# Feed-forward up-projections of a two-block transformer kernel in seven block products in place of eight

## The chip, the cores and the metric

The kernel runs on one core of a Trainium2 chip. The metric is the device time of one execution in microseconds (us), the median of three runs. Inside the core, five engines work side by side, each with its own queue of instructions in a fixed order: PE (TensorE, matrix products), DVE (VectorE), ACT (ScalarE), POOL (GpSimd) and SP, which issues the loads.

## The reference, cut to what matters

Four layers follow one another on one sequence of 512 tokens of width 1024, in 32-bit floats. The first two layers each have a mixer and a feed-forward; the change is in the two feed-forwards:

```python
def conv_ffn(x, w_up, conv_w, conv_b, w_down):      # x: 512 x 1024
    a, g = jnp.split(x @ w_up, 2, axis=-1)          # w_up: 1024 x 5632
    g = causal depthwise convolution of width 3 over tokens (g) + conv_b
    return (jax.nn.gelu(g) * a) @ w_down            # w_down: 2816 x 1024
```

(The line of the convolution is abridged.)

## The kernel before, in words

Every 32-bit value is held as a pair hi + lo of the matrix engine's rounded type, and every product is three matmuls: hi·hi, hi·lo, lo·hi (`mm3`, L273 to L278). The activations stand transposed as `xh`, `xl` (8 k-blocks of 128 rows, 512 tokens).

Weights arrive as *units* of 1 MB in one of two `raw` buffers. `pump` (L180) loads the next unit when a buffer is free and splits the next *piece* of it into hi and lo: ACT casts (L238), DVE subtracts (L242). At most five pieces exist at a time, the one that PE uses among them; `get` (L254) gives one back and fetches the next. The whole order is written out by hand: each engine works off its queue in the order in which the Python code issues.

In `ffn` (L1127) the 22 chunks of 128 hidden columns are taken two at a time: first the unit of the gate g, then that of the values a, each with two pieces (a piece is one chunk, 1024 x 128). `fm` (L282) multiplies a piece with all 512 tokens into one PSUM bank. `g_evac` (L1134) then scales on ACT (L1137), adds the two shifted taps on DVE (L1138, L1139), applies gelu on ACT (L1140); `a_evac` (L1143) multiplies on DVE (L1145) and splits the product into hi and lo (`split`, L371 and L372). After 12 chunks, and again after the other 10 (`FF_PARTS`), `tm` (L317) and `out_proj` multiply the chunks with the down-projection's weights and add into the residual. The first four chunks of a layer are done for tokens 0 to 255 and then 256 to 511 (`fms` with `split`), since the layer norm ahead of them delivers its tiles one after the other (L405 to L425).

Of the kernel before, what the change touches and what calls it, by code (L numbers as in the profile page):

```python
# [12 lines left out]
F32R = mybir.dt.float32r  # L13
# [6 lines left out]
ALPHA = (2 * 2) ** 0.25  # L20
# [8 lines left out]
SPL = 4  # L29
# [8 lines left out]
def run(gen):  # L38
    for _ in gen:
        pass  # L40
# [73 lines left out]
class Core:  # L114
# [4 lines left out]
    def __init__(self, ctx, tc, io):  # L119
        self.tc, self.nc, self.io = tc, tc.nc, io  # L120
        nc = tc.nc
        self.V, self.A, self.G, self.T = nc.vector, nc.scalar, nc.gpsimd, nc.tensor
        pool = lambda n, **k: ctx.enter_context(tc.tile_pool(name=n, **k))
        self.const = pool("const", bufs=1)
        self.wp = pool("weights", bufs=1)
        self.xp = pool("xt", bufs=1)
        self.sp = pool("slots", bufs=1)
        self.small = pool("small", bufs=4)
        self.pp = pool("psum", bufs=1, space=bass.MemoryType.PSUM)
        self.dp = pool("dram", bufs=1, space=bass.MemoryType.DRAM)  # L130
# [6 lines left out]
        self.live = deque()  # L137
        self.nm = 0
        self.pending = deque()

# [35 lines left out]
    def piece(self, u, view, a, b, direct=False):  # L176
        self.units[u]["left"] += 1
        self.plist.append((u, view, a, b, direct))

    def pump(self, split=True):  # L180
        while True:
            moved = False
            n = self.next_raw
            if n < len(self.units) and (n < self.NRAW or self.units[n - self.NRAW]["left"] == 0):
                raw = self.wp.tile([128, 2048], F32, tag="raw", name=self.name("raw"), bufs=self.NRAW)
                self.units[n]["tile"] = raw
                if self.units[n]["zero"]:
                    self.G.memset(raw[:, :self.units[n]["zero"]], 0.0)
                for dst, src in self.units[n]["srcs"]:
                    self.nc.sync.dma_start(dst(raw), src)  # L190
                    if self.loads:
                        self.loads.popleft()()
                self.next_raw += 1
                moved = True
            n = self.next_piece
            if split and n < len(self.plist) and self.room():
                u, view, a, b, direct = self.plist[n]
# [53 lines left out]
    tight = spare = extra = 0  # L251
    held = 0

    def get(self, n=1):  # L254
# [12 lines left out]
        assert len(self.live) >= n  # L267
        return [(self.live[k][1], self.live[k][2]) for k in range(n)]

    def mm3(self, out, lhs, rhs, start, stop):  # L273
        (lh, ll), (rh, rl) = lhs, rhs
        mm = self.T.matmul
        mm(out, lh, rh, start=start, stop=False)  # L276
        mm(out, lh, rl, start=False, stop=False)  # L277
        mm(out, ll, rh, start=False, stop=stop)  # L278

    step = 8  # L280

# [6 lines left out]
            if k % self.step == self.step - 1:  # L288
                yield self.step * 3 * 216 * (t1 - t0) // 512

    def fms(self, evacs, split=0):


        n = 0
        if split:
            self.flush(1)
            self.extra, self.eager = 0, False
            ws = self.get(split)
            pss = [self.ps() for _ in ws]
            for t0 in (0, 256):  # L300
                for k, (w, p) in enumerate(zip(ws, pss)):
                    if t0 or k == split - 1:
                        self.flush(3 if t0 else 2)
                    yield from self.fm(p, w, t0=t0, t1=t0 + 256)
                    if t0:
                        evacs[k](p)
                        if k == EAGER:
                            self.eager = True
                            self.pump()
            n = split  # L310
        for f in evacs[n:]:
            w, = self.get()
            p = self.ps()
            yield from self.fm(p, w)
            f(p)

    def tm(self, lhs, kpers, n, done, tail=3, pack=False, kind="mm", before=None, extra=2, middle=None):  # L317

# [779 lines left out]
        yield 500  # L1098


    FF_PARTS = (12, 10)

    def ffn_weights(self, l):
        w = self.io["ffn_w_up"][l].rearrange("(k p) n -> p k n", p=128)
        c = 0
        for part in self.FF_PARTS:
            for j in range(c, c + part, 2):
                for base in (D_FF, 0):
                    u = self.unit([(lambda r: r.rearrange("p (k n) -> p k n", k=8), w[:, :, base + 128 * j:base + 128 * j + 256])])
# [15 lines left out]
        self.ffn(1, self.pre_rms)  # L1125

    def ffn(self, l, rms=False):  # L1127
        A, V, al, fr = self.A, self.V, self.al, self.fr
        self.pool_lo = False
        par = self.par[:, l]  # L1130
        c0 = 0
        H = {}

        def g_evac(c, p):  # L1134
# [8 lines left out]
        def a_evac(c, p):  # L1143
            acc = H[c]
            V.tensor_tensor(acc, p, acc, op=MUL)  # L1145
            hi, lo = al(F32R), al(F32R)
            self.split(hi, lo, acc)
            fr(acc)
            H[c] = hi, lo

        for part in self.FF_PARTS:
            fs = []
            for j in range(c0, c0 + part, 2):
                fs += [lambda p, c=c: g_evac(c, p) for c in (j, j + 1)] + [lambda p, c=c: a_evac(c, p) for c in (j, j + 1)]
            run(self.fms(fs, split=SPL if c0 == 0 else 0))
            if c0 == 0:
                gb = self.norm_params(l, 1)
                if rms:
                    g = self.bcast(self.io["norm_pre_2"][0])
                    self.lru_params()  # L1160
                if l == 0 and self.pre_rms:
                    self.table(4)
            lhs = lambda k, i: [t[:, i * 128:i * 128 + 128] for t in H[c0 + k]]
            first = c0 == 0
            if first:
                for h in range(2):
                    run(self.tm(lhs, [2] * (part // 2), 512, lambda i, p, h=h: self.residual(i, h, p), tail=0))
            else:
                self.out_proj(lhs, [2] * (part // 2), gb, 1.0, (lambda i: self.rms_pre(i, g)) if rms else None, tail=5, extra=3)
# [966 lines left out]
```

## Time and profile before

| | |
|---|---|
| median of 3 runs | 2002.4 us (1999.98 to 2003.76) |
| the profiled execution, its own time | 1997.43 us |
| its span in the trace | 1995.5 us |
| PE busy | 1947.4 us, 98% |
| DVE, ACT, POOL busy | 50%, 41%, 21% |
| feed-forward, first layer: first load to last load of its weights | 247.8 to 622.8 us |
| feed-forward, second layer | 924.7 to 1286.8 us |

Busy time on PE is drawn from modelled ends of its matmuls, so the distance between starts tells more than the busy share. The loads run ahead of the products by up to two units.

### The profile page before, as it was taken

The numbers are of one execution on the slowest core, as the hardware profiler recorded it, in microseconds if no ns is written. First come the engines' busy times: TensorE is split into PE (matmuls) and PEld (weight loads), VectorE is DVE, ScalarE is ACT, GpSimd is POOL, SyncE is SP. The second block draws the span as 40 slices with busy tenths as digits, with TensorE's granted clock in tenths as the row PEclk, the third lists the DMA queues.
The fourth block names the chain that finished last, engine by engine and source line by source line (L and its number), as shares of the span: only waits on it lengthen the run. The fifth ranks groups of instructions, "written<-read, shape, count | busy, mean of one in ns | idle before, by whom it ended". The sixth has DMA issues, their size and how long they took to land.

```text
span 1995.5 us, 25737 instructions
## 1 busy us (share of the span) xinstructions
PE 1947.4 (98%) x10228; PEld 1623.8 (81%) x10228; DVE 991.2 (50%) x1692; ACT 817.5 (41%) x1451; POOL 417.6 (21%) x368
## 2 busy tenths in 40 slices
PE   8999989999999999999999999999998999999998
PEld 6678868888888988777888888888886888888887
DVE  3553255442444533763655344375667555455443
ACT  3455434331333344784333233256655533333331
POOL 0334441000000264474300000031443211011000
PEclk9999999999999999999999999999999999999999
DMA  6432223232323433111232423232231322222221
GB/s 199 112 115 68 93 84 101 95 127 85 105 85 123 137 99 122 54 49 64 65 116 94 137 85 105 85 106 70 71 89 70 133 85 90 90 85 90 85 75 52
DMA packets 174164, 189.22 MB, mean 95 GB/s; under 512 B 15080, under 2 KB 133662, under 8 KB 174045
## 3 DMA queue, kind: packets, MB, share of 16 engines
q1 hardware_dynamic: 158044, 165.63, 26.2%
q10 hardware_dynamic: 12064, 17.37, 2.9%
q0 software_dynamic: 3936, 4.59, 0.7%
q8 instruction: 80, 1.31, 0.3%
q14 instruction: 40, 0.32, 0.0%
HBM read 182.19 MB, written 6.65 MB: 95 GB/s over the span
## 4 chain that ended last, share of the span: by engine, by line
PE 80%; DVE 8%; ACT 3%; issue 2%; SPq 2%; DMA 2%; POOL 2%; ACTq 0%; DVEq 0%; POOLq 0%
PE p L276 24%; PE p L277 24%; PE p L278 24%; SPq L190 1%; PE p L1545 1%; PE p L1525 1%; PE p L1663 1%; SPq L851 1%; DVE s L1891 1%; POOL lo L240 1%; PE p L391 1%; PE p L786 1%; DVE s L1890 1%; PE p L366 1%; ACT hi L238 0%
## 5 line engine op out<-in xcount | busy, mean ns | idle before, releaser
L276 PE MATMUL p<-xh,hi 128*128 128x512 f32 (+1 forms) x1200 | 457.9, 382 | 0.7 <-ACT xh L371 0.7
L238 ACT CAST hi<-raw 128x1024 fp32r<-128x1024 f32 (+4 forms) x294 | 301.4, 1033 | 382.5 <-PE p L278 307.9
L277 PE MATMUL p<-xl,hi 128*128 128x512 f32 (+1 forms) x1200 | 454.3, 379 | 1.3 <-DVE xl L372 1.3
L278 PE MATMUL p<-xh,lo 128*128 128x512 f32 (+1 forms) x1200 | 454.3, 379 | 0.4 <-DVE lo L242 0.4
L242 DVE TENSOR_TENSOR lo<-raw,hi 128x1024 fp32r<-128x1024 f32 (+2 forms) x212 | 258.7, 1227 | 356.3 <-ACT hi L238 336.8
L276 PE MATMUL p<-hi,s 128*128 128x512 f32 (+1 forms) x728 | 285.7, 392 | 7.5 <-ACT s L371 4.8
L278 PE MATMUL p<-hi,s 128*128 128x512 f32 (+1 forms) x728 | 283.6, 390 | 0.0
L277 PE MATMUL p<-lo,s 128*128 128x512 f32 (+1 forms) x728 | 282.9, 389 | 0.0
L276 PEld LDWEIGHTS p<-xh,hi 128*128 128x128 f32 x1200 | 225.9, 188 | 44.7 <-ACT xh L371 1.4
L278 PEld LDWEIGHTS p<-xh,lo 128*128 128x128 f32 x1200 | 226.0, 188 | 43.1 <-DVE lo L242 0.6
L277 PEld LDWEIGHTS p<-xl,hi 128*128 128x128 f32 x1200 | 226.0, 188 | 42.8 <-DVE xl L372 2.1
L240 POOL TENSOR_TENSOR lo<-raw,hi 128x1024 fp32r<-128x1024 f32 (+3 forms) x82 | 191.2, 2339 | 329.2 <-ACT hi L238 259.6
L422 POOL TENSOR_TENSOR xtok<-xtok,b 128x512 f32<-128x512 f32 x16 | 26.1, 1629 | 712.9 <-ACT xtok L421 371.9
L276 PE MATMUL p<-hi,xh 128*128 128x512 f32 (+3 forms) x480 | 170.1, 354 | 1.5 <-ACT s L841 0.8
L277 PE MATMUL p<-lo,xh 128*128 128x512 f32 (+3 forms) x480 | 169.0, 352 | 0.5 <-DVE lo L242 0.5
L278 PE MATMUL p<-hi,xl 128*128 128x512 f32 (+3 forms) x480 | 168.8, 352 | 0.0
L276 PEld LDWEIGHTS p<-hi,s 128*128 128x128 f32 x728 | 137.1, 188 | 36.9 <-ACT s L371 6.2
L371 ACT CAST s<-s 128x512 fp32r<-128x512 f32 (+1 forms) x100 | 59.1, 597 | 260.8 <-DVE s L1145 122.7
L278 PEld LDWEIGHTS p<-hi,s 128*128 128x128 f32 x728 | 137.1, 188 | 30.0 <-DVE s L372 2.1
L277 PEld LDWEIGHTS p<-lo,s 128*128 128x128 f32 x728 | 137.1, 188 | 26.6
L276 PEld LDWEIGHTS p<-hi,xh 128*128 128x128 f32 x480 | 90.6, 189 | 14.3 <-issue 1.7
L277 PEld LDWEIGHTS p<-lo,xh 128*128 128x128 f32 x480 | 90.6, 189 | 11.7 <-DVE lo L242 0.8
(313 smaller groups left out, 2584.9 us busy)
## 6 DMA issues: line engine op xcount, KB each, us to landing
raw<-in_ffn_w_up_dram SPq DMA_DIRECT2D x44, 1024.0 KB, 5.1
raw<-in_ret_w_in_dram SPq DMA_DIRECT2D x24, 1024.0 KB, 5.1
raw<-in_ffn_w_down_dram SPq DMA_DIRECT2D x20, 1024.0 KB, 5.1
raw<-in_ev_w_in_dram SPq DMA_DIRECT2D x24, 512.0 KB, 5.3
raw<-in_lru_w_in_dram SPq DMA_DIRECT2D x24, 512.0 KB, 5.7
raw<-in_ret_w_out_dram SPq DMA_DIRECT2D x8, 1024.0 KB, 5.0
raw<-in_lru_w_out_dram SPq DMA_DIRECT2D x6, 1024.0 KB, 5.0
s<-in_od_cmp_w_dram ACTq DMA_DIRECT2D x16, 256.0 KB, 4.8
```

The costliest lines, as they stand in the source:

```text
L190: self.nc.sync.dma_start(dst(raw), src)
L238: self.A.copy(dh, x)
L240: self.G.tensor_tensor(dl, x, dh, op=SUB)
L242: self.V.tensor_tensor(dl, x, dh, op=SUB)
L276: mm(out, lh, rh, start=start, stop=False)
L277: mm(out, lh, rl, start=False, stop=False)
L278: mm(out, ll, rh, start=False, stop=stop)
L366: self.T.matmul(outs[e][:, :n], q[a][r, i * 128:i * 128 + 128], k[b][r, :n], start=j == 0, stop=j == 2)
L371: self.A.copy(hi, src)
L391: self.T.transpose(p[:, c * 128:(c + 1) * 128], halves[b][:, c * 128:(c + 1) * 128], self.ident)
L422: self.G.tensor_tensor(b, b, gb[0][:, 512:], op=MUL)
L786: T.matmul(o[:, i * 128:i * 128 + 128], st["pt"][:, k * 128:k * 128 + 128], va[k][:, h * 128:h * 128 + 128], start=k == 0, stop=k == i)
```

## The change

For every unit but the two of the first pair of chunks, the 1024 x 256 weights and the 512 tokens are cut in 2 x 2 blocks (k-halves of 512, chunks of 128; token halves of 256), and the four results are formed from seven block products in place of eight. A product is 4 k-blocks x 3 matmuls of 256 tokens. In the order of issue (`fm7`) they are: x (first half of k, first tokens), z, e, y, a second accumulation into x (here *s2*), the last product of the unit before (*s4*), a third accumulation into x (*s3*).

- **Weights.** A unit has three pieces: p0 (chunk 0 as it is), and after `post` has overwritten the raw buffer with sums on POOL (four subtractions of 128 x 512), p1 and p2. The lower right block ("corner") is split apart, for s4.
- **Activations.** Once per layer, `sum_steps` forms quarter sums of x on POOL and DVE (a11, a12, a21, a22, then s1 to s4) and splits s1 to s4.
- **Results.** x is copied out of PSUM by ACT after its first, second and third product (t0, t1, t1's second half), and DVE adds z, e and y. The evacuations then read from SBUF: the taps on DVE, and the multiplication of `a_evac` on POOL in place of DVE.
- **Parts.** The down projection follows after 6, 8 and 8 chunks in place of 12 and 10.

```diff
...
+    def seven(self, u):
+        v = lambda r: r.rearrange("p (k n) -> p k n", k=8)
+        def post(r):
+            w = v(r)
+            b11, b12, b21, b22 = w[:, :4, :128], w[:, :4, 128:], w[:, 4:, :128], w[:, 4:, 128:]
+            h, l = self.al(F32R), self.al(F32R)
+            self.split(h.rearrange("p (k n) -> p k n", k=4), l.rearrange("p (k n) -> p k n", k=4), b22)
+            self.corner.append((h, l))
+            self.G.tensor_tensor(b11, b12, b11, op=SUB)
+            self.G.tensor_tensor(b12, b22, b12, op=SUB)
+            self.G.tensor_tensor(b22, b22, b11, op=SUB)
+            self.G.tensor_tensor(b21, b21, b22, op=SUB)
+        for c, f in ((0, post), (0, None), (128, None)):
+            self.piece(u, lambda r, c=c: v(r)[:, :, c:c + 128], 8, 128, post=f)
...
-            if split and n < len(self.plist) and self.room():
+            if split and most and n < len(self.plist) and self.room():
...
+                        if post is not None:
+                            post(raw)
+                        most -= 1
...
-        self.pump()
+        self.pump(most=max(most, n - len(self.live)))
...
+            return [lambda: whole(G, "a11", 0, 0), lambda: whole(G, "a12", 0, 1)]
+        return [lambda: whole(G, "a21", 1, 0), lambda: whole(V, "a22", 1, 1),
+                lambda: comb(V, "s1", "a21", "a22", ADD, "a22"), lambda: comb(G, "s3", "a11", "a21", SUB, "a21"),
+                lambda: part("s1"), lambda: comb(G, "s2", "s1", "a11", SUB, "a11"), lambda: fr(*self.qs.pop("s1")),
+                lambda: part("s2"), lambda: comb(G, "s4", "a12", "s2", SUB, "a12"), lambda: fr(*self.qs.pop("s2")),
+                lambda: part("s3"), lambda: fr(*self.qs.pop("s3")), lambda: part("s4"), lambda: fr(*self.qs.pop("s4"))]
...
+        def mm(p, b, x, start=True):
+            for k in range(4):
+                self.mm3(p[:, :256], (b[0](k), b[1](k)), x(k), start and k == 0, k == 3, on=not start)
+            return 12 * 120
+        def blk(w, r):
+            return [lambda k, t=t: t[:, 4 * r + k] for t in w]
+        def last(u):
+            corner, y, t1, f = u
+            mm(y, [lambda k, t=t: t[:, 128 * k:128 * k + 128] for t in corner], s("s4"), False)
+            V.tensor_tensor(t1[:, :256], t1[:, :256], y[:, :256], op=ADD)
+            self.fr(*corner)
+            f(t1)
+        before = None
+        for u in range(0, len(evacs), 2):
+            w, = self.get(most=0)
+            x, z = self.ps(), self.ps()
+            t0, t1 = self.al(), self.al()
+            yield mm(x, blk(w, 0), a(0, 0))
+            A.copy(t0[:, :256], x[:, :256])
+            yield mm(z, blk(w, 1), a(0, 1))
+            V.tensor_tensor(t0[:, :256], t0[:, :256], z[:, :256], op=ADD)
+            w, = self.get(most=1)
+            y, e = self.ps(), self.ps()
+            yield mm(e, blk(w, 1), a(1, 1))
+            self.steps()
+            yield mm(y, blk(w, 0), s("s1"))
+            w, = self.get(most=1)
+            yield mm(x, blk(w, 1), s("s2"), False)
+            A.copy(t1[:, :256], x[:, :256])
+            if before:
+                last(before)
+                yield 12 * 120
+            self.pump(most=1)
+            yield mm(x, blk(w, 0), s("s3"), False)
+            A.copy(t1[:, 256:], x[:, :256])
+            V.tensor_tensor(t0[:, 256:], t1[:, 256:], e[:, :256], op=ADD)
+            V.tensor_tensor(t1[:, 256:], t1[:, 256:], y[:, :256], op=ADD)
+            evacs[u](t0)
+            before = self.corner.popleft(), y, t1, evacs[u + 1]
+        last(before)
...
-    FF_PARTS = (12, 10)
+    FF_PARTS = (6, 8, 8)
...
+                    if j:
+                        self.seven(u)
+                        continue
...
-            V.tensor_tensor(acc, p, acc, op=MUL)
+            (G if slot else V).tensor_tensor(acc, p, acc, op=MUL)
...
-            run(self.fms(fs, split=SPL if c0 == 0 else 0))
+            n = SPL if c0 == 0 else 0
+            if n:
+                run(self.fms(fs[:n], split=n, sums=True))
...
+            run(self.fm7(fs[n:]))
...
```

The queues show what moves. In them line numbers are those of the changed file. First ACT in the second part of the first layer, before: three units of two pieces; `p` are PSUM banks, `hi` cast weights, `s` slots in SBUF.

```order
L1137 ACTIVATE s717_4416<-p716_4391,par_106 128x512 [waits PE_49]
L1140 ACTIVATE s717_4416<-s717_4416 128x512 [waits DVE_49,Activation_49]
L238 CAST hi718_4421<-raw700_4285 128x1024
L1137 ACTIVATE s722_4452<-p721_4427,par_106 128x512 [waits PE_49]
L1140 ACTIVATE s722_4452<-s722_4452 128x512 [waits DVE_49,Activation_49]
L238 CAST hi723_4457<-raw710_4355 128x1024 [waits DMAHW2_49]
L371 CAST s726_4487<-s717_4416 128x512 [waits DVE_49]
L238 CAST hi728_4491<-raw710_4355 128x1024 [waits PE_49]
```

The same queue with the change, in the same part, from the evacuation of a g chunk (L1280, L1283) to the third copy from PSUM:

```order
L1280 ACTIVATE s722_4282<-s696_4064,par_106 128x512 [waits DVE_49]
L1283 ACTIVATE s722_4282<-s722_4282 128x512 [waits DVE_49,Activation_49]
L262 CAST hi723_4287<-raw703_4125 128x1024 [waits DMAHW0_49]
L511 CAST s725_4291<-raw703_4125 128x512
L450 COPY s714_4193<-p711_4190 128x256 [waits PE_49]
L511 CAST s727_4315<-s710_4185 128x512 [waits Pool_49]
L434 COPY s731_4321<-p729_4319 128x256 [waits PE_49]
L262 CAST hi733_4349<-raw703_4125 128x1024
L262 CAST hi737_4379<-raw703_4125 128x1024 [waits PE_49]
L444 COPY s732_4322<-p729_4319 128x256 [waits PE_49]
```

A cast that waits for POOL (L511 of s710, an a chunk) now stands ahead of the copy of x out of PSUM (L434).

POOL has no row in this part before; its queue with the change, at the same place:

```order
L193 TENSOR_TENSOR raw703_4125<-raw703_4125 128x4x128 [waits DMAHW0_49,DVE_49]
L194 TENSOR_TENSOR raw703_4125<-raw703_4125 128x4x128 [waits Pool_49]
L195 TENSOR_TENSOR raw703_4125<-raw703_4125 128x4x128 [waits DVE_49,Pool_49]
L196 TENSOR_TENSOR raw703_4125<-raw703_4125 128x4x128 [waits Pool_49]
L1290 TENSOR_TENSOR s710_4185<-s713_4192,s710_4185 128x512 [waits DVE_49,PE_49]
L1290 TENSOR_TENSOR s722_4282<-s714_4193,s722_4282 128x512 [waits DVE_49]
```

The multiplication that the cast of s710 waits for stands behind the four subtractions of unit raw703, whose p0 ACT casts just ahead.

PE with the change, the end of product y and the start of s2 of one unit:

```order
L303 MATMUL p717_4224<-s538_3002,lo698_4092 128x256
L301 MATMUL p711_4190<-s543_3040,hi701_4121 128x256 [waits Activation_49]
L302 MATMUL p711_4190<-s545_3042,hi701_4121 128x256
L303 MATMUL p711_4190<-s543_3040,lo702_4122 128x256
```

The second accumulation into the bank of x waits for ACT's copy. In all, PE's queue grows from 9281 rows to 10721 (rows that repeat count once).

## Rows read from the trace of the kernel before

**Rows 1.** The page, part 1: busy time, share of the span, instructions.
```profile
PE 1947.4 (98%) x10228; PEld 1623.8 (81%) x10228; DVE 991.2 (50%) x1692; ACT 817.5 (41%) x1451; POOL 417.6 (21%) x368
```
**Rows 2.** Busy time of each engine in 70 us of up-projection.
```profile
core 0: us, PE busy (x) PEld busy (x) DVE busy (x) ACT busy (x) POOL busy (x), PEclk, DMA share, GB/s
330.00:400.00 70.00, 70.00 (x310) 57.98 (x309) 36.47 (x41) 26.71 (x35) 0.00 (x0) 1.00 0.32 105
```
**Rows 3.** Timeline of PE, matmuls of 512 tokens; the first and the last of 37.
```profile
start us, us, engine line op out<-in xcount [idle before <-releaser]
379.62 0.39 PE L278 MATMUL p<-xh,lo 128*128 128x512 f32 x1
...
387.78 0.39 PE L278 MATMUL p<-xh,lo 128*128 128x512 f32 x1
```
**Rows 4.** Timeline of PE, matmuls of 256 tokens: first and last of 86.
```profile
315.78 0.28 PE L277 MATMUL p<-xl,hi 128*128 128x256 f32 x1
...
325.98 0.28 PE L278 MATMUL p<-xh,s 128*128 128x256 f32 x1
```
**Rows 5.** Timeline of ACT in the up-projection.
```profile
339.65 0.63 ACT L1140 ACTIVATE s<-s 128x512 f32<-128x512 f32 x1 [1.66 <-DVE s L1139]
340.19 1.03 ACT L238 CAST hi<-raw 128x1024 fp32r<-128x1024 f32 x1
...
343.37 0.63 ACT L371 CAST s<-s 128x512 fp32r<-128x512 f32 x1 [2.15 <-DVE s L1145]
```
**Rows 6.** Timeline of DVE in the up-projection.
```profile
336.52 1.23 DVE L242 TENSOR_TENSOR lo<-raw,hi 128x1024 fp32r<-128x1024 f32 x1 [1.70 <-ACT hi L238]
338.02 0.75 DVE L1138 SCALAR_TENSOR_TENSOR s<-p,par,s 128x511 f32<-128x511 f32 x1 [0.28 <-ACT s L1137]
338.81 0.75 DVE L1139 SCALAR_TENSOR_TENSOR s<-p,par,s 128x510 f32<-128x510 f32 x1
...
344.03 0.69 DVE L372 TENSOR_TENSOR s<-s,s 128x512 fp32r<-128x512 f32 x1 [0.69 <-ACT s L371]
```
**Rows 7.** Groups of instructions by line and shape: copies of 256 columns from PSUM.
```profile
L1533 ACT COPY s<-p 128x256 f32<-128x256 f32 x12 | 4.5, 372 | 5.3 <-PE p L1525 5.1
...
L1533 DVE COPY s<-p 128x256 f32<-128x256 f32 x12 | 5.1, 424 | 7.8 <-PE p L1525 6.9 <-POOL s L1518 0.8
```
**Rows 8.** Groups by line and shape: POOL, two operands of 512 columns.
```profile
L1970 POOL TENSOR_TENSOR s<-s,s 128x512 f32<-128x512 f32 x8 | 10.3, 1292 | 60.5 <-DVE s L1969 60.5
...
L240 POOL TENSOR_TENSOR s<-raw,s 128x512 fp32r<-128x512 f32 x8 | 10.1, 1290 | 0.0
```
**Rows 9.** Timeline of POOL during a layer norm.
```profile
947.38 5.04 POOL L240 TENSOR_TENSOR s<-raw,s 128x512 fp32r<-128x512 f32 x4
952.37 1.75 POOL L422 TENSOR_TENSOR xtok<-xtok,b 128x512 f32<-128x512 f32 x1
```
**Rows 10.** Timeline of DVE during the same layer norm.
```profile
951.10 1.86 DVE L424 SCALAR_TENSOR_TENSOR xtok<-xtok,mv,b 128x512 f32<-128x512 f32 x1
...
954.60 0.68 DVE L405 SCALAR_TENSOR_TENSOR xtok<-xtok,p 128x512 f32<-128x512 f32 x1
...
956.88 0.74 DVE L424 SCALAR_TENSOR_TENSOR xtok<-xtok,mv,b 128x512 f32<-128x512 f32 x1
```
**Rows 11.** Timeline of PE around its longest wait for another engine.
```profile
256.38 0.66 PE L994 MATMUL p<-s,s 128*64 128x128 f32 x8 [3.72 <-ACT s L985]
...
257.56 1.12 PE L994 MATMUL p<-s,s 128*64 128x128 f32 x8
...
259.65 1.12 PE L994 MATMUL p<-s,s 128*64 128x128 f32 x8
...
261.38 0.66 PE L994 MATMUL p<-s,s 128*64 128x128 f32 x8
```
**Rows 12.** Timeline of POOL ahead of the first feed-forward.
```profile
305.77 2.15 POOL L423 TENSOR_TENSOR xtok<-xtok,b 128x512 f32<-128x512 f32 x1
```
**Rows 13.** Timeline of PE: its second token half of the first four chunks begins.
```profile
314.62 0.39 PE L277 MATMUL p<-xl,hi 128*128 128x256 f32 x1 [0.34 <-DVE xl L372]
```

More of the change, by code (lines that the diff above doesn't have):

```diff
@@ L137, in __init__ @@
         self.live = deque()
+        self.corner = deque()
+        self.todo = deque()
         self.nm = 0
@@ L174, in unit, with piece, pump @@
         return len(self.units) - 1
-    def piece(self, u, view, a, b, direct=False):
+    def piece(self, u, view, a, b, direct=False, post=None):
         self.units[u]["left"] += 1
-        self.plist.append((u, view, a, b, direct))
-    def pump(self, split=True):
+        self.plist.append((u, view, a, b, direct, post))
+    def seven(self, u):
[12 more added lines that the diff above has]
+            self.piece(u, lambda r, c=c: v(r)[:, :, c:c + 128], 8, 128, post=f)
+    def pump(self, split=True, most=1000):
         while True:
@@ L289, in fm, with fms @@
                 yield self.step * 3 * 216 * (t1 - t0) // 512
-    def fms(self, evacs, split=0):
+    def fms(self, evacs, split=0, sums=False):
         n = 0
@@ L296, in fms @@
             self.flush(1)
+            if sums:
+                self.todo.extend(self.sum_steps(True))
+                self.steps()
             self.extra, self.eager = 0, False
@@ L303, in fms @@
                         self.flush(3 if t0 else 2)
+                    if t0 and k == 0 and sums:
+                        self.todo.extend(self.sum_steps(False))
+                        self.steps(4)
                     yield from self.fm(p, w, t0=t0, t1=t0 + 256)
@@ L306, in fms @@
                         evacs[k](p)
+                        if k:
+                            self.steps(3)
                         if k == EAGER:
@@ L315, in fms, with quarter, sum_steps, whole @@
             f(p)
+    def quarter(self, x, th, kh):
+        return x[:, 4 * kh:4 * kh + 4, 256 * th:256 * th + 256]
+    def sum_steps(self, early):
+        V, G, al, fr = self.V, self.G, self.al, self.fr
+        v = lambda t: t.rearrange("p (k n) -> p k n", k=2)
+        if early:
+            self.qs, self.sums = {}, {}
+        def whole(E, n, th, kh):
+            self.qs[n] = [al(), al()]
+            for c, t in enumerate(self.qs[n]):
+                x = [self.quarter(y, th, kh)[:, 2 * c:2 * c + 2] for y in (self.xh, self.xl)]
+                E.tensor_tensor(v(t), x[0], x[1], op=ADD)
+        def comb(E, n, a, b, op, out):
+            for x, y, t in zip(self.qs[a], self.qs[b], self.qs[out]):
+                E.tensor_tensor(t, x, y, op=op)
+            self.qs[n] = self.qs.pop(out)
+        def part(n):
+            hs, ls = [al(F32R), al(F32R)], [al(F32R), al(F32R)]
+            for h, l, t in zip(hs, ls, self.qs[n]):
+                self.split(h, l, t)
+            self.sums[n] = hs, ls
+        if early:
+            return [lambda: whole(G, "a11", 0, 0), lambda: whole(G, "a12", 0, 1)]
[4 more added lines that the diff above has]
+                lambda: part("s3"), lambda: fr(*self.qs.pop("s3")), lambda: part("s4"), lambda: fr(*self.qs.pop("s4"))]
@@ new lines, in steps, with fr_sums, fm7, a @@
+    def steps(self, n=1000):
+        while n and self.todo:
+            self.todo.popleft()()
+            n -= 1
+    def fr_sums(self):
+        for hs, ls in self.sums.values():
+            self.fr(*hs, *ls)
+    def fm7(self, evacs):
+        V, A = self.V, self.A
+        def a(th, kh):
+            return lambda k: (self.quarter(self.xh, th, kh)[:, k], self.quarter(self.xl, th, kh)[:, k])
+        def s(n):
+            hs, ls = self.sums[n]
+            return lambda k: tuple(t[k // 2][:, 256 * (k % 2):256 * (k % 2) + 256] for t in (hs, ls))
+        def mm(p, b, x, start=True):
[22 more added lines that the diff above has]
+            yield mm(e, blk(w, 1), a(1, 1))
+            self.steps()
+            yield mm(y, blk(w, 0), s("s1"))
[13 more added lines that the diff above has]
+        last(before)
@@ L1141, in g_evac, with a_evac @@
             H[c] = acc
-        def a_evac(c, p):
+            if slot:
+                fr(p)
+        def a_evac(c, p, slot=False):
             acc = H[c]
-            V.tensor_tensor(acc, p, acc, op=MUL)
+            (G if slot else V).tensor_tensor(acc, p, acc, op=MUL)
+            if slot:
+                fr(p)
             hi, lo = al(F32R), al(F32R)
@@ L1162, in ffn @@
                     self.table(4)
+            run(self.fm7(fs[n:]))
+            if c0 + part == 22:
+                self.fr_sums()
             lhs = lambda k, i: [t[:, i * 128:i * 128 + 128] for t in H[c0 + k]]
-            first = c0 == 0
-            if first:
+            alpha = ALPHA if c0 == 0 else 1.0
+            if c0 + part < 22:
                 for h in range(2):
-                    run(self.tm(lhs, [2] * (part // 2), 512, lambda i, p, h=h: self.residual(i, h, p), tail=0))
+                    run(self.tm(lhs, [2] * (part // 2), 512, lambda i, p, h=h: self.residual(i, h, p, alpha), tail=0))
             else:
-                self.out_proj(lhs, [2] * (part // 2), gb, 1.0, (lambda i: self.rms_pre(i, g)) if rms else None, tail=5, extra=3)
+                self.out_proj(lhs, [2] * (part // 2), gb, 1.0, (lambda i: self.rms_pre(i, g)) if rms else None, tail=4, extra=3)
             for c in range(c0, c0 + part):
```

18 lines of the change are left out of this document (9 added, 9 removed).

## Prediction

> **What bounds the kernel now.** The page's busy times come first: PE is busy 98% of the span, the others half or less [rows 1]. Then one stretch of up-projection: of 70 us PE is busy 70, at a granted clock of 1.00 (2.4 GHz); DVE has 36 us of work, ACT 27, POOL none [rows 2]. So there PE's own rate is the time, and the others have room. The rate is read from starts, not from durations, which overlap: 36 steps in 8.16 us are 0.2267 us for a matmul of 512 tokens [rows 3], 85 steps in 10.20 us are 0.120 us for one of 256 [rows 4]. Half the tokens cost 53% of the time.
>
> **What PE gains.** A unit now takes 2 chunks x 8 k-blocks x 3 x 0.2267 = 10.88 us. With the change it is 7 products x 12 x 0.120 = 10.08 us (1.44 us a product). Ten of eleven chunk pairs have two such units, in two layers: 40 units, and PE's queue grows by just the 40 x 36 rows that this means. The gain is 40 x 0.80 = 32 us: the upper bound.
> The Trainium skill (TensorE: Matmul & The Clock Gate, "Back-to-back issue gap") gives N/2.4 + 2.5 ns, 215.8 and 109.2 ns, and so 1.19 us a unit and 47 us in all. The rows are 11 ns above that for either width, and the measurement decides.
>
> **What it adds beside PE.** Prices: cast of 1024 columns on ACT 1.03, of 512 0.63 (I take 0.62), gelu or scaling from SBUF 0.63 [rows 5]; subtraction of 1024 on DVE 1.23, a tap 0.75, 512 columns 0.69 [rows 6]; 256 columns from PSUM 0.37 on ACT, 0.42 on DVE [rows 7]; 512 columns on POOL 1.29 [rows 8]. A hand-over between engines is 0.03 to 0.09 us (a cast ends at 344.00 and DVE starts at 344.03, a tap ends at 339.56 and gelu starts at 339.65) [rows 5, 6]; I take 0.05.
> For a g unit and its a unit: POOL does 8 subtractions and 2 multiplications, 12.9 us. DVE's operations with two operands in SBUF are 6 x 1.23, two corners and two halves of chunks at 0.69, and four taps at 0.75 (before they read PSUM): 13.1 us. Those 26.0 us would hide in 20.2 us of PE if the two engines were free of each other. They are not: while POOL ran four operations back to back, DVE's L424 with two SBUF operands took 1.86 us, alone 0.74; POOL's next took 1.75 instead of 1.29; L405, which reads PSUM, took 0.68 beside POOL's work [rows 8 to 10]. So each waits for the other to end. I take it as a full exclusion; the other bound is none.
>
> **The queues.** The order rows show what stands behind what. ACT's copy of x (L434) must come before PE's s2, and 7.2 us of PE's work separate the end of s4 in one unit from s2 in the next. In that stretch ACT's queue holds the gelu of the chunk that s4 finished, the cast of p0 for the unit after the next, and the cast of an a chunk, which waits for POOL's multiplication, which stands behind the four subtractions that wait for p0. In steady state this closes to a ring over the three engines:
> - g unit's last chunk to a copy: gelu 0.63, cast p0 1.03, subtraction 1.23, corner 0.69, POOL 4 x 1.29 and 1.29, cast 0.62, copy 0.37, cast p1 1.03, subtractions p1 and p2 2.46, adding y 0.42: 14.9 us.
> - on from there: POOL's multiplication 1.29, cast 0.62, cast p0 1.03, subtraction 1.23, corner 0.69, POOL 4 x 1.29 with two taps in between 1.50, cast p1 1.03, subtractions 2.46, adding y 0.42, scaling 0.63, two taps 1.50: 17.6 us, and gelu again.
>
> Together 32.5, with 15 hand-overs 33.2 us for a pair of units, against 21.8 now. PE waits in this ring some 7.9 us ahead of s2 of each g unit and 5 us elsewhere. The five pieces do not hide it: a lead delays a ring, it does not shorten it. Without the exclusion the same walk gives 30.6.
>
> **The sum.** A part of 8 units begins with its pieces ready: 9.3 and 12.2 us for the first pair, three rings of 33.2, and 3.9 at the end, since the last s4 waits for the copy that ACT has behind a gelu and a cast: 125.0 us in place of 8 x 10.88 = 87.0, **+38.0**. There are four such parts, +152.
> The first part of a layer has 4 units, and 12 quarter sums on POOL ahead. POOL is free 6.7 us before the second token half begins (305.77 + 2.15 against 314.62) [rows 12, 13]. From there on the walk to s3 of the first unit is: 15 POOL operations, 19.4 us; DVE's a22 and s1, p1 and p2 in between, 5.2; two taps and gelu 2.1; halves of s1 to s4 with the last two a chunks between, 10.1; z, p0 and corner of the next unit 2.3; its subtractions 5.2; a cast and the copy 1.4: 45.7, with hand-overs 46.6. That is 39.9 after the half began; without any wait s3 would start at 18.8. Behind it p0 and p1 are cast in one unit, with the subtractions in between, as the lead is one piece shorter: units of 15.8, 19.1 and 17.9. The part with its 11.5 us of split chunks is 95.2 us where 55.0 stood: **+40.2**, twice, +80.
> Clock: after 3.72 us of waiting PE still ran a group of 8 in 0.66 us, then from 257.56 to 260.77 the same in 1.12, then in 0.66 again [rows 11]: 3.2 us at half rate, 1.2 GHz for 2.4. Behind a long wait s2 and s4 would take 1.6 us longer, of which the ring has 0.45 in hand. I take 1.15 for each of 12 rings, +14; bounds 0 and 1.6 for each of 26 long waits, 42.
> The third down projection adds 8 residual additions on DVE a layer, beside products of 8 x 12 x 0.2267 = 21.8 us on PE in each half: 0; uncovered they would be 8 x 0.69 = 6 us.
> Sum: 152 + 80 + 14 = +246. Against the profiled execution, 1997.4, that is 2243; the median of the three runs is 5 us above it, so I forecast **2248 us**.
>
> **Rivals.**
> 1. *No exclusion*, the queues alone (0.22). Rows 10 show it for a layer norm only, with other operands. Ring 30.6, parts +30.0 and +33.2: +186, 2002.4 + 186 = 2188. With hand-overs of 0.03 and POOL at 1.26 it is +174. The Trainium skill (GPSIMD Engine Reference, "Specifications") says that POOL's access to SBUF is shared with VectorE and contends with instructions with two SBUF inputs; by that rule my forecast, not this rival, holds.
> 2. *Exclusion alone* (0.08): the lead lets the queues run smoothly, and 26.0 us for a pair stay where 21.8 stood: 20 x 4.3 = +85, 2088. Against it: the ring holds no slack that a lead could use.
> 3. *Faster* (0.04): POOL's work goes under. Place: the four subtractions ahead of the multiplication. The ring has ten POOL operations, so it equals today's 21.8 once they take 1.29 - 11.4/10 = 0.15 us each, and shorter ones give up to 32 us: 1971. Only then, or if POOL's a chunk passed the subtractions, would it decide; no row of POOL with two operands of 512 is near that, and its order is fixed.
> 4. *Clock and restarts cost in full* (0.06): +28 on the forecast, 2276; with POOL at 1.35 some 2290.
> That the change does not do what it says is excluded by the count of rows.
>
> **How the numbers follow.** The forecast has 0.60. It and the first and fourth rival hold 0.88, from 2176 (174 above 2002.4) to 2290. I let the range run from 2165 to 2300; left out are rivals 2 and 3 at 0.12 and what I have not thought of. A measurement of this kernel tells about 0.2% (4 us) from no change. Faster by more needs rival 3: 0.04; within it, where gains and ring happen to cancel, 0.01; slower 0.95.
>
> **What would show it.** PE busy falls to some 85% of the span, its waits are named after ACT's copy lines (L434, L444) and DVE; units take about 18 and 15 us in the second and third parts, and 29 us in the first unit of each layer. POOL's four subtractions are 1.29 us each, and DVE's subtractions beside them are stretched; the granted clock drops after the longest waits. I am wrong if PE's starts show units near 10.1 us, if POOL's operations are far shorter, or if ACT's casts of a chunks do not wait for POOL.

## The result and the profile after

The changed kernel takes **2261.49 us** (2259.72 to 2262.52, 4 runs), the kernel before 2003.08 (1999.98 to 2004.31, 4 runs): a ratio of 1.129, 95% interval 1.127 to 1.131. Slower, as forecast (2248), and inside the range. The profiled execution took 2262.5 us (its span in the trace is 2260.6), 265.1 us more than the 1997.4 of before.

The page after: part 1, the granted clock of part 2, and the shares of the chain that ended last.
```profile
PE 2001.8 (89%) x11668; PEld 1739.4 (77%) x11668; DVE 1154.9 (51%) x1932; ACT 921.8 (41%) x1667; POOL 731.6 (32%) x592
...
PEclk9999997988988999999979989889999999999999
...
PE 55%; DVE 16%; POOL 10%; ACT 9%; issue 6%; DMA 2%; SPq 2%; ACTq 0%; POOLq 0%; DVEq 0%
```
PE is busy 89% where it was 98% [rows 1]. Its busy time rose all the same, though it has less to compute: part of it ran at half rate. In the chain that sets the end POOL and DVE have 10% and 16%, where they had 2% and 8% before:
```profile
PE 80%; DVE 8%; ACT 3%; issue 2%; SPq 2%; DMA 2%; POOL 2%; ACTq 0%; DVEq 0%; POOLq 0%
```

Waits of PE in the changed kernel: line, who ended it, total, times, longest.
```profile
PE p L301 <- ACT s L434: 120.5, 30, 6.9
PE p L301 <- ACT s L444: 40.4, 10, 11.8
PE p L301 <- DVE s L452: 31.3, 6, 5.2
PE p L301 <- DVE s L1282: 9.9, 2, 5.1
PE p L301 <- DVE s L1290: 6.7, 2, 3.4
```
These five make 209 us; in the up-projections of before PE had no such waits. ACT's two copy lines are first, and L452 ends each of the six parts.

Busy time by stretch: first part, second and third part of the first layer.
```profile
core 0: us, PE busy (x) PEld busy (x) DVE busy (x) ACT busy (x) POOL busy (x), PEclk, DMA share, GB/s
332.00:413.00 81.00, 51.43 (x329) 49.95 (x328) 42.55 (x57) 31.64 (x51) 26.00 (x19) 0.79 0.29 95
447.00:575.00 128.00, 92.25 (x674) 90.39 (x673) 68.04 (x86) 49.35 (x77) 46.56 (x34) 0.86 0.22 71
619.00:749.00 130.00, 94.72 (x674) 92.81 (x673) 68.30 (x86) 49.39 (x77) 46.83 (x34) 0.84 0.22 70
```
Before, such a stretch had PE busy from end to end at a clock of 1.00 [rows 2]. Now no engine is full, not even DVE and POOL taken together (114.6 of 128): that is how a ring of waits looks.

**The ring** can be read off 11 us of two timelines. ACT first:
```profile
538.80 0.63 ACT L1283 ACTIVATE s<-s 128x512 f32<-128x512 f32 x1 [1.66 <-DVE s L1282]
539.34 1.03 ACT L262 CAST hi<-raw 128x1024 fp32r<-128x1024 f32 x1
540.28 0.62 ACT L511 CAST s<-raw 128x512 fp32r<-128x512 f32 x1
540.80 0.36 ACT L450 COPY s<-p 128x256 f32<-128x256 f32 x1
548.64 0.62 ACT L511 CAST s<-s 128x512 fp32r<-128x512 f32 x1 [7.48 <-POOL s L1290]
549.17 0.37 ACT L434 COPY s<-p 128x256 f32<-128x256 f32 x1
```
POOL in the same stretch:
```profile
541.71 1.66 POOL L193 TENSOR_TENSOR raw<-raw 128x512 f32<-128x512 f32 x1 [10.39 <-DVE lo L266]
543.45 1.26 POOL L194 TENSOR_TENSOR raw<-raw 128x512 f32<-128x512 f32 x1
544.79 1.26 POOL L195 TENSOR_TENSOR raw<-raw 128x512 f32<-128x512 f32 x1
546.13 1.26 POOL L196 TENSOR_TENSOR raw<-raw 128x512 f32<-128x512 f32 x1
547.35 1.26 POOL L1290 TENSOR_TENSOR s<-s,s 128x512 f32<-128x512 f32 x1
```
Gelu, cast of p0, subtraction on DVE, four subtractions and the multiplication on POOL, the cast of the a chunk, and behind it, in the same queue, the copy of x: 10.4 us from gelu to copy, in the order forecast. The copy needs none of this. ACT stood idle for 7.48 us ahead of it, for an instruction that is in front of it by order of issue alone.

PE behind that copy: s2, and where the clock came back.
```profile
549.59 0.58 PE L301 MATMUL p<-s,hi 128*128 128x256 f32 x1 [6.54 <-ACT s L434]
...
551.04 0.41 PE L301 MATMUL p<-s,hi 128*128 128x256 f32 x1
551.25 0.41 PE L302 MATMUL p<-s,hi 128*128 128x256 f32 x1
...
553.28 0.28 PE L301 MATMUL p<-s,s 128*128 128x256 f32 x1
553.40 0.28 PE L302 MATMUL p<-s,s 128*128 128x256 f32 x1
```
The starts lie 0.21 us apart after the wait and 0.12 from 552.9 on: half rate (1.2 GHz) for 3 us, then full rate (2.4).

**Where the 265 us are**, from the starts on PE:

| | before | after | more |
|---|---|---|---|
| four parts of 8 units, each | 87.0 | 128.0, 129.9, 127.3, 129.9 | 166.9 |
| whole units of the first part, each layer | 43.5 | 82.0, 89.3 | 84.3 |
| down projections, each layer | 117.0 | 120.2, 119.5 | 5.8 |
| everything else | | | 8.1 |

Counted another way, the six stretches of up-projection hold 209 us of waits, 74 us that matmuls lost at half rate (some 690 of 3350 steps), less the 32 us that PE gained: 251, the first two lines. Of the last line 3.6 us stood at 92 us already, ahead of every changed instruction; the start of the program differs by up to 5 us from kernel to kernel below too, so single totals are read with that in mind and lengths of parts are preferred. Run 4 below, which differs from before in its parts alone, is itself 6.5 us above the 1997.4, with up-projections equal to before's within 0.1 us: most of the last line has nothing to do with the seven products.

### The profile page after: what moved, and what is told of

It is laid out like the page before. It is cut to its first block, busy times and chain, and to the rows that moved or that the text cites. A ratio compares the mean times of both kernels' runs of the same rounds, so it can differ in the third digit from the quotient of the medians.

```text
span 2260.6 us, 29402 instructions
## 1 busy us (share of the span) xinstructions
PE 2001.8 (89%) x11668; PEld 1739.4 (77%) x11668; DVE 1154.9 (51%) x1932; ACT 921.8 (41%) x1667; POOL 731.6 (32%) x592
## 4 chain that ended last, share of the span: by engine, by line
PE 55%; DVE 16%; POOL 10%; ACT 9%; issue 6%; DMA 2%; SPq 2%; ACTq 0%; POOLq 0%; DVEq 0%
PE p L301 16%; PE p L302 15%; PE p L303 15%; DVE lo L266 4%; ACT hi L262 3%; POOL raw L193 2%; DVE s L1281 2%; DVE s L1282 2%; POOL s L1290 2%; POOL raw L195 1%; POOL raw L196 1%; SPq L211 1%; POOL raw L194 1%; PE p L1697 1%; PE p L1677 1%
## 5 line engine op out<-in xcount | busy, mean ns | idle before, releaser
L262 ACT CAST hi<-raw 128x1024 fp32r<-128x1024 f32 (+3 forms) x334 | 339.8, 1033 | 416.9 <-PE p L303 263.3
L266 DVE TENSOR_TENSOR lo<-raw,hi 128x1024 fp32r<-128x1024 f32 (+2 forms) x252 | 307.7, 1237 | 370.0 <-ACT hi L262 367.2
L301 PE MATMUL p<-xh,hi 128*128 128x256 f32 (+1 forms) x1040 | 352.0, 338 | 18.4 <-DVE s L1282 9.9
L302 PE MATMUL p<-xl,hi 128*128 128x256 f32 (+1 forms) x1040 | 347.7, 334 | 2.1 <-DVE xl L512 2.0
L303 PE MATMUL p<-xh,lo 128*128 128x256 f32 (+1 forms) x1040 | 347.0, 334 | 0.0
L301 PE MATMUL p<-s,hi 128*128 128x256 f32 (+1 forms) x536 | 177.4, 331 | 161.3 <-ACT s L434 120.5
L301 PEld LDWEIGHTS p<-s,hi 128*128 128x128 f32 x536 | 116.3, 217 | 172.2 <-ACT s L434 126.8
L511 ACT CAST s<-s 128x512 fp32r<-128x512 f32 (+1 forms) x116 | 67.2, 596 | 320.3 <-POOL s L1290 176.5
L193 POOL TENSOR_TENSOR raw<-raw 128x512 f32<-128x512 f32 x40 | 66.0, 1651 | 348.2 <-DVE lo L266 348.2
L302 PE MATMUL p<-s,hi 128*128 128x256 f32 (+1 forms) x536 | 171.5, 320 | 0.4 <-DVE s L512 0.3
L303 PE MATMUL p<-s,lo 128*128 128x256 f32 (+1 forms) x536 | 170.9, 319 | 0.0
L301 PEld LDWEIGHTS p<-hi,s 128*128 128x128 f32 x728 | 139.0, 191 | 37.6 <-ACT s L511 6.4
```

Source lines behind the costliest of these rows:

```text
L193: self.G.tensor_tensor(b11, b12, b11, op=SUB)
L262: self.A.copy(dh, x)
L266: self.V.tensor_tensor(dl, x, dh, op=SUB)
L301: mm(out, lh, rh, start=start, stop=False, skip_group_check=on)
L302: mm(out, lh, rl, start=False, stop=False, skip_group_check=on)
L303: mm(out, ll, rh, start=False, stop=stop, skip_group_check=on)
```

## The experiments

After the result I walked the queues again on paper, as in the prediction, but with s2 and the product behind it as slow after a long wait as the trace shows them. For a part of 8 units that gives 131.3 us with full exclusion between POOL and DVE's two-operand work and 123.4 with none; 128.8 is the mean measured. The expectations below use these walks; they are estimates made by hand, and their working is not shown. Runs 1 to 7 were timed once each. Lengths of parts are taken from the start of x in the first unit to the start of the product behind the last s4.

**1. Subtractions on DVE** (post_dve): in seven(), four lines
```diff
-            self.G.tensor_tensor(b11, b12, b11, op=SUB)
+            self.V.tensor_tensor(b11, b12, b11, op=SUB)
...
```


> The four subtractions of a unit's weight blocks are done on DVE in place of POOL (0.69 us each in place of 1.29); all else as in the changed kernel. This tells exclusion from none. With full exclusion between POOL and DVE's operations on two SBUF operands, the queue walk for a part of 8 units goes from 131.3 (with the half-rate clock after waits) to 127.1 us, and the first part of a layer from 98.1 to 89.2: 4 x -4.2 and 2 x -8.9 make -35, so about 2227 us. Without exclusion the same walk has the part rise from 123.4 to 127.1, since DVE is made longer and POOL was no hindrance, and the first part fall by 7.7: +15 - 15, so about 2261 us, no change.

Measured: 2236.7 us, parts 125.9 to 127.0, first parts about 7 us shorter. The parts agree with the walk (127.1) to 0.8 us on average, and fell where a walk without exclusion says they must rise by 3.7. DVE got 40 x 4 x 0.69 = 110 us more work and the kernel became faster. The rival without exclusion does not stand, but the fall is 2.5 us a part and not 4.2.

**2. Multiplication on DVE** (mul_dve): in a_evac
```diff
-            (G if slot else V).tensor_tensor(acc, p, acc, op=MUL)
+            V.tensor_tensor(acc, p, acc, op=MUL)
```


> The multiplication of the a chunks goes back from POOL to DVE, so that it no longer stands behind the four subtractions; all else as in the changed kernel. Ring over three queues with exclusion: a part of 8 units goes from 131.3 to 121.8 us, the first part by -0.9, in all -40, about 2221 us, and ACT's casts of a chunks no longer wait for POOL. Ring without exclusion: 123.4 to 110.1, in all about -55, 2206 us. If not the ring but the sum of busy time of the two engines set the pace, only 20 pairs x 2 x (1.29 - 0.69) = -24 would come back, 2237 us.

Measured: 2210.4 us, parts 116.9 to 117.1, first parts unchanged. Waits of PE in this run:
```profile
PE p L301 <- ACT s L444: 61.0, 22, 11.4
PE p L301 <- ACT s L434: 56.9, 27, 4.0
PE p L301 <- DVE s L452: 31.3, 6, 5.2
```
The wait for L434 halves, and its longest goes from 6.9 to 4.0, while that for the second copy, L444, rises from 40.4 to 61.0. 51 us came back where the sum of busy times would give 24: it was the multiplication's place in POOL's queue that cost, more than its length. The size lies between the two rings (40 and 55), nearer to the one without exclusion. So exclusion is there (run 1) but is not full; the section on the prediction takes that up.

**3. No subtractions** (no_post): the same four lines are taken out.

> Left out: the four subtractions of weight blocks in each of 40 units (the products then take the plain blocks, so the values are not those of the reference). POOL keeps the multiplication of a chunks and the sums of x. Ring with exclusion: a part of 8 units goes from 131.3 to 103.6, the first part from 98.1 to 75.9, in all 4 x -27.7 + 2 x -22.2 = -155, about 2106 us. Without exclusion -19.8 and -19.8, about -119, 2142 us. In both the time stays over the kernel before: what is left is the ring over ACT and DVE and the sums in the first part. If the chain of subtractions were all of the loss, it would fall under 2003.

Measured: 2125.4 us, parts 104.8 to 106.5 (walk 103.6), first parts some 20 and 23 us shorter: -136, again between -155 and -119. The four subtractions are half of the loss, and a part without them is still 18 us longer than 87.0. Here PE's waits are short, and the clock fell even so. PE behind one of them:
```profile
476.61 0.38 PE L297 MATMUL p<-s,hi 128*128 128x256 f32 x1 [1.94 <-ACT s L430]
476.84 0.28 PE L298 MATMUL p<-s,hi 128*128 128x256 f32 x1
476.95 0.28 PE L299 MATMUL p<-s,lo 128*128 128x256 f32 x1
...
478.04 0.42 PE L298 MATMUL p<-s,hi 128*128 128x256 f32 x1
478.25 0.41 PE L299 MATMUL p<-s,lo 128*128 128x256 f32 x1
...
481.20 0.28 PE L298 MATMUL p<-s,hi 128*128 128x256 f32 x1
```
The wait is over at full rate (0.12 from start to start), then come 3.4 us at 0.21. Waits of 1.93 and 1.98 us earlier in the same part were followed by none.

**4. Eight products in three parts** (eight_688): seven() is not called, and fms does all units; FF_PARTS stays (6, 8, 8).

> Eight products everywhere, as in the kernel before, but the feed-forward parts of 6, 8, 8, so a third down projection in each layer. My theory: it costs nothing by itself, 2003 us within 3; the 1.7 and 0.8 us by which the first two down projections of the changed kernel are longer than 5.44 us a chunk come from the half-rate clock after the wait that ends each part. Rival: residual additions or piece casts at the extra seam cost some 3 us a layer, 2009 us.

Measured: 2003.9 us beside 2003.2 for the kernel before. Its down projections take 32.64 us for 6 chunks and 43.52 for 8, where the changed kernel has 34.3 and 44.3. The third down projection costs nothing, as forecast; the changed kernel starts each of them at half rate, behind the wait for L452.

**5. Work in the waits** (warm): in fm7, behind product y
```diff
+            for _ in range(3 if before and u % 4 == 0 else 0):
+                yield mm(e, blk(w, 1), a(1, 1))
```


> Ahead of s2 in every second unit of a part (where PE waits about 6.6 us), PE computes product e three times more, 4.3 us of work whose values are the same, so that it does not stand still; there are 3 such places in a part of 8 units and 1 in a first part, 14 in all. By my forecast the half-rate clock behind such a wait lengthens the ring by 1.15 us: 14 x 1.15 = -16, about 2245 us, although PE gets 60 us more work. Rival, the half rate costs in full what the products behind the wait lose (s2 2.72 and s4 2.0 us on average in place of 1.44): 14 x 1.8 = -25, 2236 us. Second rival, ACT's and DVE's queues set the end whatever PE's clock is: 0, 2261 us. In all three the wait itself shrinks by 4.3 us at each of the 14 places.

Measured: 2250.8 us, but 4.9 us of the 10.7 stand ahead of the first feed-forward. In the six stretches waits fell by 56 us, work rose by 60, and the loss at half rate went from 74 to 64 us: some 6 us in all. As totals the forecast of 16 us and the rivals of 25 and 0 are all out. What half rate costs at one place is not settled by that, for it did not go away at all the filled places: in each part of 8 the clock fell even so behind one or two of the three shortened waits in front of s2 (2.63 and 2.18 us), and did not behind one of 2.35. In the four parts of 8, which hold 12 of the 14 places, 10 us less were lost at half rate and the time fell by 8.

**6. Copies first** (copies_first): as run 1, and in fm7
```diff
+        def even(u):
+            u[4](u[5])
...
             if before:
+                even(before)
                 last(before)
...
-            evacs[u](t0)
-            before = self.corner.popleft(), y, t1, evacs[u + 1]
+            before = self.corner.popleft(), y, t1, evacs[u + 1], evacs[u], t0
+        even(before)
         last(before)
```


> The four subtractions on DVE as in post_dve, and the evacuation of a unit's first chunk (scaling, taps and gelu, or multiplication, cast and rest) is issued behind the next unit's copies of x (L434, L444) in place of ahead of them: no engine gets more or less work than in post_dve. Ring through ACT's queue: a part of 8 units falls from 126.4 (measured in post_dve) to the 108.7 of the walk, the first part by about half as much: 4 x -17.7 + 2 x -9 from 2236.7, about 2148 us, and PE's waits for L434 shrink to some 3 us or less. Rival, the sum of the work that excludes each other (DVE's two-operand work and POOL's) sets the pace: order alone changes nothing, 2237 us.

Measured: 2159.9 us, parts 105.9 to 107.3. The first parts, for which some 9 us were forecast, did not change (99.2 and 109.0 where run 1 has 100.4 and 108.2). Waits of PE:
```profile
PE p L301 <- DVE s L456: 77.3, 25, 6.7
PE p L301 <- ACT s L447: 24.8, 10, 9.1
...
PE p L301 <- ACT s L437: 8.7, 10, 1.5
```
The wait for the first copy (L437 here) is 8.7 us where run 1 has 109.9 for the same line. No engine's work differs from run 1; 19 us of each part were order alone. The rest of the wait is now DVE's: for a pair of units it has 13.1 us of two-operand work, 8 x 0.42 of additions from PSUM and 8 x 0.69 of subtractions, 22.0 us beside 20.2 on PE. No order makes that fit.

**7. Sums in time** (sums_early): the first part goes by eight products, its multiplications go back to DVE, and one step of the sums of x stands behind each of its last eight chunks.
```diff
-                    if j:
+                    if c:
...
             yield from self.fm(p, w)
             f(p)
+            self.steps(1)
...
-            run(self.fm7(fs[n:]))
+            if n:
+                self.todo.extend(self.sum_steps())
+                run(self.fms(fs[n:]))
+                self.steps()
+            else:
+                run(self.fm7(fs))
```


> First part of each layer by eight products, its loss taken out alone: the sums of x are made one step behind each of its last eight chunks; second and third parts as in the changed kernel. Theory: the two first parts lose 38.5 and 45.8 us to the chain of sums on POOL ahead of s2 and s3, and that falls away whole, with some 1.2 us at each layer norm: 2261.5 - 87, about 2175 us; the parts of 8 units stay at 127 to 130. Rival, the sums only move the wait, since POOL's 12 operations and the rest beside them hold up the evacuations of the first part: less than 40 of the 87 come back, over 2220 us.

Measured: 2177.4 us; the four parts are 129.7 to 129.9, and the first parts are as long as with eight products in run 4 (69.4 us with their split chunks). PE's wait for the second copy (L444 in the changed kernel, L439 here) falls from 40.4 us to 1.9:
```profile
PE p L301 <- ACT s L429: 118.8, 28, 6.9
PE p L301 <- DVE s L447: 20.9, 4, 5.2
...
PE p L301 <- ACT s L439: 1.9, 4, 0.5
```
The loss of the first parts is gone, and 12 operations of POOL hide when they have eight chunks of time. That the sums alone were the loss is not shown, for this run takes the four subtractions out of the first part too. Without these (run 3) 20 and 23 us of it were gone already, and in the changed kernel they end the wait for s3. ACT ahead of it:
```profile
354.44 1.04 ACT L262 CAST hi<-raw 128x1024 fp32r<-128x1024 f32 x1 [6.58 <-POOL raw L196]
355.39 0.37 ACT L444 COPY s<-p 128x256 f32<-128x256 f32 x1
```
The copy of x stands behind the cast of the next unit's p1, which waits for that unit's last subtraction. DVE's last halves of the sums (to 347.2 us) stand ahead of this chain, so both have a share.

**8. Seven products where they fit** (g_seven): subtractions and multiplications on DVE, sums as in run 7, seven products for the g units of the second and third parts only.
```diff
-                    if j:
+                    if c and base:
...
+            yield mm(y, blk(w, 0), s("s1"))
+            self.pump(most=1)
+            w, w1 = self.live[1][1:], w
+            yield mm(x, blk(w, 1), s("s2"), False)
+            A.copy(t1[:, :256], x[:, :256])
+            yield mm(e, blk(w1, 1), a(1, 1))
+            self.held = 2
...
+            for k in (2, 3):
+                w, = self.get(most=1)
+                p = self.ps()
+                yield from self.fm(p, w)
+                if k == 2:
+                    evacs[u](t0)
+                    last((self.corner.popleft(), y, t1, evacs[u + 1]))
+                    yield 12 * 120
+                evacs[u + k](p)
```


> A version meant to keep PE's gain: seven products in the g units of the second and third parts alone (4 of 8 units), a units and the first part by eight; sums of x made during the first part, one step behind each chunk; subtractions and multiplications on DVE; product e between s2 and s3, and the first chunk's evacuation behind the next unit's first product. In the walk of the queues PE never waits: 16 units x 0.80 = -13 against the kernel before, about 1990 us. With all durations beside PE 10% longer the walk gives -3, 20% longer +18 (2020 us). If the sums of x hold DVE up in the first part, some us more; then waits for pieces show there.

Measured: **1990.7 us** (1988.1 to 1992.4, 4 runs) against 2002.6 of the kernel before beside it; ratio 0.9946, interval 0.9930 to 0.9963. Busy time in its second part:
```profile
core 0: us, PE busy (x) PEld busy (x) DVE busy (x) ACT busy (x) POOL busy (x), PEclk, DMA share, GB/s
430.00:517.00 87.00, 87.00 (x480) 76.07 (x479) 57.65 (x74) 35.52 (x49) 0.00 (x0) 1.00 0.32 109
```
PE is full again at a clock of 1.00 [rows 2], with DVE at 58 of 87 us. A part takes 84.0 us, and 3.0 of 87.0 for 4 units are 0.76 a unit: the gain that the prediction put at 0.80. This version beats both kernels.

**9. The same with POOL** (g_seven_pool): run 8 with the four subtractions on POOL.

> The kernel of g_seven with the four subtractions on POOL, which has nothing else to do in these parts (5.2 us in a pair of 21 us). With exclusion between POOL and DVE's two-operand work the walk of a part of 8 units goes from 83.8 to 87.6 us, 4 x 3.8 = +15, about 2006 us; without exclusion to 85.7 (the longer subtraction alone), +8, about 1998 us. If POOL's spare time were free, 1991 us.

Measured: 2010.7 us (2010.0 to 2015.5, 5 runs), ratio 1.0048, interval 1.0032 to 1.0064; the first of the four parts takes 87.6 us, the others 89.0. The first subtraction (shortest, middle and longest time in ns) and PE's longest group of waits in this run:
```profile
L193 POOL TENSOR_TENSOR raw<-raw x16: 1617/1624/1683, 385.8 to 1258.1; 128x512 f32<-128x512 f32 x16
```
```profile
PE p L301 <- ACT s L428: 12.2, 8, 2.4
```
The first two parts:
```profile
404.60:492.20 87.60, 84.52 (x529) 76.44 (x528) 51.28 (x70) 39.07 (x57) 16.46 (x12) 1.00 0.29 97
535.70:624.70 89.00, 85.98 (x529) 77.89 (x529) 51.45 (x70) 38.97 (x57) 16.45 (x12) 0.98 0.28 95
```
PE waits 3.0 to 3.1 us in every part. In the first the clock stayed at 1.00, and its length is that of the walk with exclusion (3.8 us more; 1.9 without); in the other three it fell behind the second wait, which makes 1.4 us more. 16 x 4 operations, moved to an engine that has nothing else to do there, make the difference between 0.5% faster and 0.5% slower than before.

## Why the prediction was right

- **PE's gain**, 0.80 a unit, 32 us: right. Products start 1.44 us apart wherever PE does not wait, and run 8 got 0.76.
- **The ring**: right in its members and order (the timelines above, runs 2 and 6). Forecast 33.2 us for a pair and 1.15 for the clock; from s2 to the s2 two units on it is 33.0 to 35.8, and 31.4 and 32.1 for the last of a part. Units of about 18 and 15 were forecast with no clock; in the second part they are 15.9, 19.1, 15.5, 18.4.
- **Parts of 8**: +152 and +14 for the clock were forecast, +166.9 measured. That the two agree so closely is luck: the exclusion was taken too large and the clock too small, by about as much (below).
- **First parts**: +80 forecast, 38.5 and 45.8 measured. The walk put s3 of the first unit 39.9 us behind the start of the second token half; it came at 36.5 and 42.6 (counted from the matmul of rows 13). The units after it, 15.8, 19.1, 17.9 by the walk, took 16.6, 18.6, 19.1 in the first layer. What the walk did not name are two waits ahead of it for PSUM banks that DVE still read (L1282, L1290), and in the second layer a table load on ACT and 30 short DVE operations (L1946 to L1965, 1136.8 to 1142.7 us), which stand ahead of the subtraction that POOL's four wait for: most of the 6.1 us by which s3 came later there.
- **Third down projection**, 0: right (run 4). The 5.8 us in the changed kernel belong to the clock.
- **Clock**: the cause was right, the term too small. The second parts of the changed kernel lost 11.6 and 10.6 us at half rate and took 128.0 and 127.3; the third parts lost 14.0 each and took 129.9, with the same waits (35.3 to 36.0 us in all four): 0.8 us of length for each us lost. Run 9 (1.4 us for 1.5 lost) and run 5 (8 for 10) say much the same, so little of it hid inside the waits. By the walks the clock as the trace shows it is worth 6.3 us a part (131.3 against the 125.0 of the forecast without it), where the forecast had 3.5. No run takes the half rate away whole, so this size stays an estimate.
- **Exclusion**: the step that was mis-sized. The forecast takes it as full. Three subtractions on POOL beside two taps on DVE:
```profile
526.70 1.28 POOL L194 TENSOR_TENSOR raw<-raw 128x512 f32<-128x512 f32 x1
528.06 1.59 POOL L195 TENSOR_TENSOR raw<-raw 128x512 f32<-128x512 f32 x1
529.73 1.59 POOL L196 TENSOR_TENSOR raw<-raw 128x512 f32<-128x512 f32 x1
```
```profile
526.69 1.84 DVE L1281 SCALAR_TENSOR_TENSOR s<-s,par,s 128x511 f32<-128x511 f32 x1 [0.43 <-ACT s L1280]
528.57 1.63 DVE L1282 SCALAR_TENSOR_TENSOR s<-s,par,s 128x510 f32<-128x510 f32 x1
```
The three take 4.62 us from start to end where they take 3.94 with DVE quiet (543.45 to 547.39, above): each tap holds POOL up by 0.34 us, not by its 0.75. The taps, which take 0.75 alone [rows 6], take 1.84 and 1.63. So DVE loses most of a subtraction's time (0.9 to 1.1 of 1.26 us), POOL less than half of a tap's. The Trainium skill (SBUF — State Buffer, "SBUF: two separate sides") says that whichever of the two starts first has the shared port for the whole instruction and the other blocks; these rows agree that DVE waits, and show less than the whole instruction for POOL. The walks, against the lengths of a part of 8 units:

| | full exclusion | none | measured |
|---|---|---|---|
| changed kernel | 131.3 | 123.4 | 128.8 |
| post_dve | 127.1 | 127.1 | 126.3 |
| mul_dve | 121.8 | 110.1 | 117.0 |
| no_post | 103.6 | 103.6 | 105.3 |
| copies_first | 108.7 | 106.9 | 106.9 |
| g_seven | 83.8 | 83.8 | 84.0 |
| g_seven_pool | 87.6 | 85.7 | 87.6, then 89.0 three times |

Where POOL has little or nothing to do the walk is right within 2 us; where both work hard, the truth lies between the two bounds in two cases, at the lower in one (copies_first, with little of POOL left) and at the upper in the last where the clock did not fall; the 1.4 us above it in the other three parts are the clock, which that walk leaves out (run 9).

- **Rivals**: without exclusion (2188): out, by runs 1 and 9 and by the taps above. Exclusion alone, queues running ahead (2088): out, since run 6 gained 77 us by order alone. POOL's work under cover (1971): its operations take 1.26 to 1.29 us, not 0.15. The clock in full (2276): not excluded. The 2261.5 measured lies midway between it and the 2248, and the clock cost more than the 14 us that the forecast gave it.

Against its own profiled execution the forecast was +246, measured were +265.1. Of the 19 us between, 5 are in the parts, 5.8 in down projections that begin at half rate, put at zero, and 8.1 outside the feed-forward, most of which run 4 shows as well. The medians lie only 13.5 apart, since the profiled execution of before was 5 us under its median. So the forecast is right in place and mechanism, and so near in its number partly by luck, as two sizes were off in opposite ways: the exclusion too large, what follows from the clock too small.

## What to carry to other kernels

Fewer products on the full engine help only as far as the work that feeds them fits beside it in order as well as in sum: here 16 of the 40 units, with their subtractions and multiplications on one engine, gave 0.5%, and all 40 cost 13%. Write down each engine's queue between two products, and look for an instruction that stands, by order of issue alone, behind one that waits for another engine; moving such copies forward gave 77 us (run 6 against run 1) with no work saved. An idle engine is no free place for a chain: ask what it takes from its neighbour, and how long the chain gets.

## What the runs showed of the hardware

- A wait of 1.94 us in otherwise dense work was followed by 3.4 us at 1.2 GHz, and waits of 1.93 and 1.98 us like it by none (run 3). In run 9 waits of 2.28 to 2.32 us were followed by half rate and one of 2.36 was not. The length of one wait does not tell it.
- Filling 14 waits with 4.3 us of real products each took away 10 of 74 us lost at half rate: the clock fell behind some of the shortened waits too (2.2 and 2.6 us, run 5).
- Parts of one kernel whose waits are alike (35.3 to 36.0 us) differ in length by 0.8 us for each us that they lose at half rate (10.6 to 14.0 us; second and third parts of the changed kernel).
- POOL's two-operand subtraction of 512 columns takes 1.26 us alone and 1.59 beside a DVE tap; the tap goes from 0.75 to 1.63 and 1.84. An addition with one operand in PSUM took 0.41 us beside POOL's L193 (L451 at 525.39 us), and the same with POOL quiet (L436 at 549.90).
